# A scratch of rotated queries and keys laid out row by row, with six loads a half-head where there were ten

## The chip, the cores and the metric

The kernel runs on one core of a Trainium2 chip. The metric is device time in microseconds (us) from start to end of one execution, as a median of several. The core has five engines that run side by side, each through its own list of instructions in a fixed order: PE (TensorE, matrix products), DVE (VectorE), ACT (ScalarE), POOL (GpSimd) and SP (SyncE). In this kernel SP does no arithmetic: it issues every transfer between the chip's large memory (DRAM here) and the on-chip buffers, one after another. The transfers themselves run on 16 DMA engines. PE writes into eight accumulation banks that ACT and DVE read out.

## What is computed

One decoder layer over 1024 positions of width 2048, in float32. After a norm, one projection gives the columns of eight attention heads (queries, keys, values, gate) and of eight recurrent blocks. Each attention head has two score maps (m = 0, 1) of 64 dimensions, and the rotation acts on halves of 32 (t = 0, 1). Cut to what matters here:

```python
h = rms_norm(x, norm_gain[l]); proj = h @ w_in[l]
q, k, v, g_attn, xr, g_rec = jnp.split(proj, SPLITS, axis=-1)
q = rope(q.reshape(bsz, seq, 8, 2, 64), cos, sin)
k = rope(k.reshape(bsz, seq, 8, 2, 64), cos, sin)
s = einsum('bhmqd,bhmkd->bhmqk', q, k) * 64 ** -0.5      # causal
p = softmax(s); w = p[:, :, 0] - lam * p[:, :, 1]
o = w @ v; o = rms_norm(o, subln_gain) * 0.8 * silu(g_attn)
r = rg_lru(causal_conv(xr)) * silu(g_rec)
x = x + concat(o, r) @ w_out[l]
return rms_norm(x, final_gain)
```

To keep the precision of float32 in faster passes, the kernel splits each operand into a high and a low part (hi + lo) and adds up products of the parts.

## The kernel before

The class `Trunk` builds everything. It counts in slots: a slot (`tick`) is the work of one weight tile on PE, and generators that were spawned earlier (rope, scores, out_weights and so on) put their instructions into the slots as these go by. A scheduler then fixes the order on each engine, so neighbours can stand some places off from the order of the code; `order` fences below show the final one. Buffers are 89 tiles of 128 x 512 float32, handed out in turn.

There are three stages.

- **Projection** (`projection`, L659 on PE), to about 1100 us in the profile. In its last segment `rope(h, c4)` rotates queries and keys of head h. For each half l of the positions (512 columns) it ends with four tiles of 128 x 512: the high and low parts for t = 0 (`t2`, `t1`) and t = 1 (`pa`, `pb`). The 128 rows of each are four groups of 32: query m = 0, query m = 1, key m = 0, key m = 1. The four tiles are written whole to a scratch in DRAM, `fs[h, l]` of shape [4, 128, 512], in the order hi t0, hi t1, lo t0, lo t1 (L802).
- **Attention beside the recurrent half of the output projection** (`rec_half`), from about 1110 to 1745 us. The output projection runs 256 slots of three matmuls each (L1078, L1079, L1080: hi x hi, hi x lo, lo x hi), with weights that `out_weights` loads (L176, `b<-w_out`), copies on ACT (L189) and subtracts on POOL (L190). Between the slots, `scores` and `weighted` do the attention of 16 half-heads (8 heads, 2 halves of the positions). `head_load(h, l)` brings a half-head's operands in: keys k (2 tiles), queries q (4 tiles) and values (2 tiles). `score` multiplies them (L869, L870), DVE masks (L874), ACT takes the exponential (L881), PE turns the weights (L996), ACT and DVE split them (L1005, L1006), and PE applies them to the values (L1018, L1020, L1021). `head_out` norms the result (L967, L975, L978).
- **The attention half of the output projection** (`att_half`), to the end.

What each score tile holds matters for the change. The contraction of a score runs over 128 rows, which is four blocks of 32. The key tile of map m holds (hi t0, hi t1, lo t0, lo t1), block after block. The first query tile holds (hi t0, hi t1, hi t0, hi t1) and the second (lo t0, lo t1, lo t0, lo t1); L869 takes the first and L870 adds the second, so that all four products of parts are summed. A query tile is filled by two loads, each of 64 rows.

All transfers are issued by SP in its one order, by `self.load` (its line is L176) and `self.store` (L180); a load whose target tile is still being read waits there, and so does everything behind it. Besides, a transfer takes one of eight counters in turn and waits until the one eight places ahead of it on that counter has landed.

Of the kernel before, what the change touches and what calls it, by code (L numbers as in the profile page):

```python
# [13 lines left out]
F32 = mybir.dt.float32  # L14
# [7 lines left out]
P = 128  # L22
# [3 lines left out]
HALF = 512  # L26
# [95 lines left out]
class Trunk:  # L122
# [659 lines left out]
    def rope(self, h, c4):  # L782
        nc = self.nc
        for l in range(2):
            pa, pb = c4.pop(f"1{l + 1}"), c4.pop(f"2{l + 1}")
            t1, t2 = self.alloc(), self.alloc()
            sin, cos = self.sin[l], self.cos[l]
            self.tt(t1.f, pa.f, cos, ALU.mult)
            self.tt(t2.f, pb.f, sin, ALU.mult)
            yield 1  # L790
            self.tt(t1.f, t1.f, t2.f, ALU.subtract)
            self.split(t1.f, t2, t1)
            yield 2
            self.tt(pa.f, pa.f, sin, ALU.mult)
            self.tt(pb.f, pb.f, cos, ALU.mult)
            yield 2
            self.tt(pb.f, pb.f, pa.f, ALU.add)
            self.split(pb.f, pa, pb)
            yield 2
            fs = self.fs[h, l] = self.dram.tile([4, P, HALF], F32, name=self.nm("fs"))  # L800
            for i, b in enumerate((t2, pa, t1, pb)):
                nc.sync.dma_start(fs[i], b.f)  # L802
            self.rel(t1, t2, pa, pb)
            yield 2

# [30 lines left out]
    def head_load(self, h, l):  # L836
        k, q, v = [], [], []
        for m in range(2):
            kk = self.allocr()
            self.load(kk.f, self.fs[h, l][:, 64 + 32 * m:96 + 32 * m, :])  # L840
            k.append(kk)
        for i in (0, 2):
            for m in range(2):
                t = self.allocr()
                for j in range(2):
                    self.load(t.f[64 * j:64 * j + 64], self.fs[h, l][i:i + 2, 32 * m:32 * m + 32, :])
                q.append(t)
        for d in self.vsc[h, l]:
            t = self.allocr()
            self.load(t.f, d)  # L850
            v.append(t)
        self.hd[h, l] = (k, q, v)
# [382 lines left out]
```

## Time and profile before

| | us |
|---|---|
| median of 3 runs (1943.13 to 1944.86) | 1944.32 |
| profiled execution, its own time | 1941.15 |
| its span, first to last instruction | 1939.4 |
| PE busy / DVE busy / ACT busy / POOL busy | 1600.9 / 1273.9 / 815.3 / 632.7 |
| stretch 1110 to 1745 us (attention) | 635 |

Times in rows of the profile are microseconds of the profiled execution, from its first instruction. "Busy" is the time in which an engine has an instruction running; PE's matmuls are pipelined, so a busy PE is not one at its peak, and the clock column shows how much of TensorE's full clock was granted (1.00 is 2.4 GHz, 0.50 is 1.2 GHz). "DMA share" is the mean busy share of the 16 DMA engines. A wait is put down to the instruction whose completion ended it. "SPq" is the SP queue; its duration is how long SP was held by a transfer's issue, not how long the bytes took.

### The profile page before, as it was taken

The page shows a single profiled execution, that of the slowest core. Times are in us where ns is not written, and L with a number is a line of the kernel's source. Part 1 is how long each engine was busy: PE and PEld are TensorE (multiplying, and loading weights), DVE is VectorE, ACT ScalarE, POOL GpSimd, SP SyncE. Part 2 cuts the span into 40 slices and gives each one's busy share as a digit, 9 for nine tenths or more (in the row PEclk, how much of TensorE's full clock was granted, in tenths as well). Part 3 has the DMA queues.
Part 4 walks back from the last instruction along what each step waited for, and adds up shares of the span by engine and source line. Part 5 has one row for each costly group of instructions (what it writes and reads, how often), then busy time and mean ns, then how long its engine had stood idle before and what let it go on. Part 6 is the DMA issues. An engine that isn't in the chain of part 4 may idle for free. (4 is left out here: it accounts for less than half of the span.)

```text
span 1939.4 us, 22308 instructions
## 1 busy us (share of the span) xinstructions
PE 1600.9 (83%) x7140; PEld 1296.3 (67%) x7140; DVE 1273.9 (66%) x2120; ACT 815.3 (42%) x1462; POOL 632.7 (33%) x486
## 2 busy tenths in 40 slices
PE   7988988989889889999999945664857777599998
PEld 5767877767677667777777734553645556477876
DVE  9776798777887878989999823443634455373412
ACT  6444445453454455333333312333433343364442
POOL 3574323332333345232343310211211122147381
PEclk9999999999899899999999967787969788799999
DMA  6766423233232337455555724434444434455552
GB/s 240 250 209 217 160 81 123 90 125 112 85 122 90 111 104 268 166 188 177 197 204 190 253 87 149 137 134 144 148 160 141 136 103 141 130 178 169 184 197 87
DMA packets 164565, 299.98 MB, mean 155 GB/s; under 512 B 17376, under 2 KB 19552, under 8 KB 164448
## 3 DMA queue, kind: packets, MB, share of 16 engines
q1 hardware_dynamic: 164448, 298.56, 46.1%
q8 instruction: 56, 0.92, 0.2%
q14 instruction: 61, 0.50, 0.1%
HBM read 206.22 MB, written 92.27 MB: 154 GB/s over the span
## 5 line engine op out<-in xcount | busy, mean ns | idle before, releaser
L659 PE MATMUL pp<-b,b 128*128 128x512 f32 x3612 | 886.2, 403 | 104.8 <-DVE b L193 84.9
L659 PEld LDWEIGHTS pp<-b,b 128*128 128x128 f32 x3612 | 697.9, 195 | 275.2 <-DVE b L193 99.8
L190 POOL TENSOR_TENSOR b<-b,b 128x512 fp32r<-128x512 f32 x288 | 452.4, 1584 | 772.8 <-ACT b L189 437.4
L189 ACT CAST b<-b 128x512 fp32r<-128x512 f32 x592 | 355.1, 619 | 725.4 <-DVE b L193 277.9
L190 DVE TENSOR_TENSOR b<-b,b 128x512 fp32r<-128x512 f32 x304 | 243.3, 812 | 66.0 <-ACT b L189 56.8
L193 DVE TENSOR_TENSOR b<-b,b 128x512 f32<-128x512 f32 x340 | 256.3, 768 | 19.1 <-POOL b L190 12.4
L1078 PE MATMUL pq<-b,b 128*128 128x512 f32 x512 | 211.0, 412 | 19.1 <-ACT b L189 18.6
L1079 PE MATMUL pq<-b,b 128*128 128x512 f32 x512 | 209.7, 410 | 2.9 <-POOL b L190 2.8
L1080 PE MATMUL pq<-b,b 128*128 128x512 f32 x512 | 208.9, 408 | 3.0 <-DVE b L190 3.0
L193 DVE TENSOR_TENSOR b<-pp,b 128x512 f32<-128x512 f32 x215 | 146.9, 683 | 61.0 <-PE pp L659 48.2
L193 POOL TENSOR_TENSOR b<-b,b 128x512 f32<-128x512 f32 (+1 forms) x56 | 74.9, 1338 | 282.0 <-ACT b L733 89.8
L193 DVE TENSOR_TENSOR b<-pq,b 128x512 f32<-128x512 f32 x89 | 61.0, 686 | 150.6 <-PE pq L1080 125.1
L874 DVE CUSTOM_DVE_ANT_0 sw<-sw,mask 128x256 f32<-128x256 f32 (+7 forms) x128 | 97.0, 763 | 66.2 <-PE sw L870 64.8
L1006 DVE TENSOR_TENSOR b<-pq,b 128x512 fp32r<-128x512 f32 (+1 forms) x80 | 50.7, 634 | 118.4 <-ACT b L1005 117.3
L881 ACT ACTIVATE wide<-sw,mx 128x256 f32<-128x256 f32 (+7 forms) x128 | 93.8, 739 | 79.2 <-DVE mx L877 78.8
L1078 PEld LDWEIGHTS pq<-b,b 128*128 128x128 f32 x512 | 100.7, 197 | 36.5 <-ACT b L189 19.9
L1018 PE MATMUL pq<-b,b 128*128 128x256 f32 x160 | 51.5, 322 | 77.2 <-ACT b L1005 43.4
L1079 PEld LDWEIGHTS pq<-b,b 128*128 128x128 f32 x512 | 100.6, 196 | 21.4 <-POOL b L190 5.4
L1080 PEld LDWEIGHTS pq<-b,b 128*128 128x128 f32 x512 | 100.2, 196 | 21.1 <-DVE b L190 4.6
L193 DVE TENSOR_TENSOR b<-b,wide 128x512 f32<-128x512 f32 x120 | 99.0, 839 | 9.6 <-ACT wide L1148 9.0
L659 PE MATMUL pq<-b,b 128*128 128x512 f32 x420 | 103.8, 393 | 1.3 <-POOL b L190 1.0
L869 PE MATMUL sw<-b,b 128*128 128x512 f32 (+2 forms) x192 | 76.9, 402 | 28.4 <-ACT wide L881 21.9
(148 smaller groups left out, 1638.9 us busy)
## 6 DMA issues: line engine op xcount, KB each, us to landing
b<-w_in SPq DMA_DIRECT2D x192, 256.0 KB
b<-w_out SPq DMA_DIRECT2D x128, 256.0 KB
pt<-b SPq DMA_DIRECT2D x96, 256.0 KB
b<-pt SPq DMA_DIRECT2D x96, 256.0 KB
b<-xt SPq DMA_DIRECT2D x72, 256.0 KB
fs<-b SPq DMA_DIRECT2D x64, 256.0 KB
b<-fs SPq DMA_DIRECT2D x128, 128.0 KB
b<-yd SPq DMA_DIRECT2D x32, 256.0 KB
```

Source lines behind the costliest of these rows:

```text
L189: self.nc.scalar.copy(hi.r, x)
L190: (eng or self.nc.vector).tensor_tensor(out=lo.r, in0=x, in1=hi.f, op=ALU.subtract)
L193: (eng or self.nc.vector).tensor_tensor(out=out, in0=a, in1=b, op=op)
L659: nc.tensor.matmul(acc, lhsT=a.r[:, s], rhs=b.r, start=FIRST[pi] and qq == 0 and j == 0, stop=qq == 3 and j == 2, skip_group_check=True)
L869: nc.tensor.matmul(o, lhsT=q[m].r[:, qs], rhs=kk, start=True, stop=False)
L874: nc.vector.tensor_tensor_reduce(out=s, in0=s, in1=self.mask[:, 896 - off:896 - off + cols], scale=1.0, scalar=NEG, op0=ALU.add, op1=ALU.m ...
L881: nc.scalar.activation(p[:, :cols], self.swide[m][:, :cols], AF.Exp, scale=QK ** -0.5, bias=mx[:, m:m + 1], accum_out=sm[:, m:m + 1])
L1006: nc.vector.tensor_tensor(out=wl.r[:, first:], in0=self.tr[:, first:], in1=wh.f[:, first:], op=ALU.subtract)
L1018: nc.tensor.matmul(o, lhsT=vh.r[:, vs], rhs=wh.r[:, cs], start=(k2 == 0 and i == 0), stop=False)
L1078: nc.tensor.matmul(acc, lhsT=mh.r[:, s], rhs=wh.r, start=kt == 0, stop=False)
L1079: nc.tensor.matmul(acc, lhsT=mh.r[:, s], rhs=wl.r, start=False, stop=False)
L1080: nc.tensor.matmul(acc, lhsT=ml.r[:, s], rhs=wh.r, start=False, stop=kt == 7)
```

## The change

The scratch of a half-head gets the shape [4, 32, 6, 512]: first the group (query m = 0, query m = 1, key m = 0, key m = 1), then the row within the group, then a place for up to six blocks side by side. The four tiles go to places 0 to 3 of all four groups (four stores of 128 rows, each row of 2 KB now 12 KB from the next), and the two high tiles once more to places 4 and 5 of the query groups (two further stores of 64 rows). A half-head is then loaded by six transfers of 128 rows: each key tile reads places 0 to 3 of its group, the first query tile of a map places 0 to 3 and the second places 2 to 5, so that 4 x 512 numbers that lie in one run in DRAM become four neighbouring rows on the chip. The rows of a contraction are thus interleaved (row, block) where they were (block, row), in keys and queries alike. The first query tile now holds hi and lo beside the keys' hi and lo, the second lo and hi: the same four products are summed, in other pairs.

```diff
-            fs = self.fs[h, l] = self.dram.tile([4, P, HALF], F32, name=self.nm("fs"))
+            fs = self.fs[h, l] = self.dram.tile([4, 32, 6, HALF], F32, name=self.nm("fs"))
             for i, b in enumerate((t2, pa, t1, pb)):
-                nc.sync.dma_start(fs[i], b.f)
+                nc.sync.dma_start(fs[:, :, i].rearrange("g r c -> (g r) c"), b.f)
+            for i, b in enumerate((t2, pa)):
+                nc.sync.dma_start(fs[:2, :, 4 + i].rearrange("g r c -> (g r) c"), b.f[:64])
             self.rel(t1, t2, pa, pb)
...
         for m in range(2):
             kk = self.allocr()
-            self.load(kk.f, self.fs[h, l][:, 64 + 32 * m:96 + 32 * m, :])
+            self.load(kk.f, self.fs[h, l][2 + m, :, :4])
             k.append(kk)
         for i in (0, 2):
             for m in range(2):
                 t = self.allocr()
-                for j in range(2):
-                    self.load(t.f[64 * j:64 * j + 64], self.fs[h, l][i:i + 2, 32 * m:32 * m + 32, :])
+                self.load(t.f, self.fs[h, l][m, :, i:i + 4])
                 q.append(t)
```

On the DRAM side, the access pattern of a key load goes from 4 steps of 32 rows of 512 to 32 steps of 4 rows of 512; that of a query load from 2 steps of 32 rows (64 rows in all) to 32 steps of 4 (128 rows). The new stores have 128 or 64 steps of one row.

The instructions on PE, DVE, ACT and POOL are the same in number and kind; the scheduler shifts some of them by a few places in the attention stage. SP changes as follows. First the stores of head 0 in the projection, on SP, before (fs is the scratch, pt partial results, vs values):

```order
L802 DMA fs_6768<-b_6725 128x512
L802 DMA fs_6768<-b_6724 128x512
L176 DMA b_6819<-pt_2562 128x512
L176 DMA b_6815<-w_in 128x512
L176 DMA b_6817<-w_in 128x512
L176 DMA b_6851<-pt_2584 128x512
L802 DMA fs_6768<-b_6499 128x512
L802 DMA fs_6768<-b_6669 128x512
L180 DMA vs_6791<-b_6519 128x512
```

And now:

```order
L802 DMA fs_6768<-b_6725 128x512
L804 DMA fs_6768<-b_6725 64x512
L802 DMA fs_6768<-b_6724 128x512
L176 DMA b_6817<-w_in 128x512
L176 DMA b_6821<-pt_2562 128x512
L176 DMA b_6819<-w_in 128x512
L176 DMA b_6853<-pt_2584 128x512
L802 DMA fs_6768<-b_6499 128x512
L802 DMA fs_6768<-b_6669 128x512
L804 DMA fs_6768<-b_6499 64x512
L180 DMA vs_6793<-b_6519 128x512
```

The two stores of 64 rows (L804) stand between the others, each by the store of the same tile.

Second, the loads of one half-head in the attention stage, on SP, before; x is the residual input, ys a stored sum of the output projection, ms a stored head output, and "x2" marks two rows that follow each other (it is the head load that the trace has at 1248.83 us):

```order
L176 DMA b_10212<-x 128x512
L176 DMA b_10225<-fs_7380 128x1x512
L176 DMA b_10227<-fs_7380 128x1x512
L176 DMA b_10229<-fs_7380 64x1x512 x2
L176 DMA b_10232<-fs_7380 64x1x512 x2
L176 DMA b_10235<-fs_7380 64x1x512 x2
L176 DMA b_10238<-fs_7380 64x1x512 x2
L176 DMA b_10241<-vs_7552 128x512
L176 DMA b_10243<-vs_7553 128x512
L180 DMA ys_10211<-b_10093 128x512
L180 DMA ms_10209<-b_10155 128x512
L176 DMA b_10331<-w_out 128x512
```

And now:

```order
L176 DMA b_10228<-x 128x512
L176 DMA b_10241<-fs_7388 128x1x512
L176 DMA b_10243<-fs_7388 128x1x512
L176 DMA b_10245<-fs_7388 128x1x512
L176 DMA b_10247<-fs_7388 128x1x512
L176 DMA b_10249<-fs_7388 128x1x512
L176 DMA b_10251<-fs_7388 128x1x512
L176 DMA b_10253<-vs_7564 128x512
L176 DMA b_10255<-vs_7565 128x512
L176 DMA b_10343<-w_out 128x512
L176 DMA b_10357<-w_out 128x512
L176 DMA b_10370<-w_out 128x512
```

Eight loads of 64 rows have become four of 128, the weights stand behind the values as before, and the stores of ys and ms have moved behind the weights.

## Rows read from the trace of the kernel before

**Rows 1.** The page: its span, and in 40 equal slices of 48.5 us PE's busy share and the granted clock, in tenths.

```profile
span 1939.4 us, 22308 instructions
...
PE   7988988989889889999999945664857777599998
...
PEclk9999999999899899999999967787969788799999
```

**Rows 2.** Stretches of the span: bounds and length in us, then busy us and number of instructions of PE, PEld (weight loads), DVE, ACT and POOL, granted clock, DMA share, GB/s. First the last segment of the projection, then the attention stage, then four stretches of it in which PE is hardly ever idle, then one in which SP issues loads from fs and nothing else, last one in which the loads are the recurrent half's operands and weights.

```profile
806.00:1110.00 304.00, 289.21 (x1258) 232.90 (x1257) 281.56 (x426) 109.32 (x191) 96.87 (x47) 0.98 0.60 202
1110.00:1745.00 635.00, 419.96 (x2127) 342.86 (x2126) 288.58 (x751) 237.13 (x487) 123.48 (x148) 0.81 0.41 139
1360.00:1397.00 37.00, 36.72 (x212) 31.03 (x210) 27.22 (x73) 20.41 (x43) 8.47 (x12) 1.00 0.48 162
1570.00:1604.00 34.00, 32.30 (x187) 26.97 (x186) 25.49 (x60) 20.99 (x41) 11.10 (x12) 1.00 0.38 125
1616.00:1647.00 31.00, 29.81 (x166) 24.08 (x165) 22.11 (x64) 16.31 (x38) 8.94 (x11) 0.96 0.36 119
1690.00:1740.00 50.00, 49.16 (x270) 40.15 (x269) 36.36 (x97) 32.41 (x68) 14.90 (x14) 0.96 0.47 154
1255.20:1269.60 14.40, 14.40 (x77) 12.44 (x76) 10.19 (x23) 4.78 (x11) 1.48 (x2) 0.83 0.14 55
1090.00:1110.00 20.00, 19.14 (x87) 15.53 (x86) 17.47 (x25) 7.20 (x12) 7.95 (x7) 1.00 0.96 331
```

**Rows 3.** Whom PE waited for from 1110 to 1745 us, longest first: total us, times, longest us.

```profile
PE pq L1018 <- ACT b L1005: 43.4, 4, 18.7
PE pq L978 <- DVE hs L975: 38.0, 2, 27.6
PE pq L996 <- DVE b L1006: 24.3, 5, 12.0
PE sw L869 <- ACT wide L881: 21.9, 9, 9.3
PE pq L1018 <- issue: 21.3, 2, 10.9
PE pq L1078 <- ACT b L189: 18.2, 2, 18.0
PE sw L870 <- DMA b<-fs: 16.8, 3, 10.6
PE pq L1018 <- POOL b L1004: 12.3, 1, 12.3
PE sw L869 <- DMA b<-fs: 6.1, 2, 4.1
```

**Rows 4.** The timeline around 1191 to 1217 us, of SP (three rows), ACT and PE: start and duration in us, then the instruction, its count and in brackets the idle time before it and what ended it.

```profile
1191.95 9.50 SPq L176 DMA_DIRECT2D b<-fs  x3
1201.55 2.92 SPq L176 DMA_DIRECT2D b<-vs  x2
1204.52 1.74 SPq L176 DMA_DIRECT2D b<-w_out  x3
...
1215.70 1.87 ACT L189 CAST b<-b 128x512 fp32r<-128x512 f32 x3 [18.30 <-DMA b<-w_out]
...
1216.37 0.80 PE L1078 MATMUL pq<-b,b 128*128 128x512 f32 x1 [17.96 <-ACT b L189]
```

**Rows 5.** The chain of work that ended last, between 1190 and 1290 us: start, length in us, what. A DMA's piece runs from its issue to its landing.

```profile
1205.16 11.15 DMA b<-w_out
...
1241.53 10.81 DMA b<-vs
...
1262.15 2.44 SPq L176
1264.63 2.44 SPq L176
...
1274.58 9.70 DMA b<-w_out
```

**Rows 6.** The timeline of SP at the head load of the order fence above.

```profile
1248.83 20.74 SPq L176 DMA_DIRECT2D b<-fs  x10
1269.61 2.97 SPq L176 DMA_DIRECT2D b<-vs  x2
```

**Rows 7.** Issues on SP by the tensor they move: count, then the time that an issue held SP in ns (least, median, longest) and the us at which the first and the last started. Loads from fs, stores to fs, stores of the output and loads of x; the last two move 128 rows of 2 KB that lie 8 KB apart in DRAM.

```profile
L176 SPq DMA_DIRECT2D b<-fs x160: 484/993/4552, 1110.2 to 1669.4; - x160
L802 SPq DMA_DIRECT2D fs<-b x64: 319/320/1192, 806.8 to 1098.5; - x64
...
L1165 SPq DMA_DIRECT2D out<-b x32: 332/391/1256, 1828.6 to 1935.2; - x32
...
L176 SPq DMA_DIRECT2D b<-x x32: 327/382/1342, 1109.6 to 1691.3; - x32
```

**Rows 8.** The third matmul of a slot (L1080) alone, in the attention stage and in its four dense stretches: length, PE busy us and count, PEld, clock, DMA share, GB/s.

```profile
1110.00:1745.00 635.00, 108.12 (x257) 51.81 (x256) 0.81 0.41 139
1360.00:1397.00 37.00, 10.24 (x26) 4.89 (x26) 1.00 0.48 162
1616.00:1647.00 31.00, 7.96 (x19) 3.72 (x19) 0.96 0.36 119
1690.00:1740.00 50.00, 12.53 (x30) 6.02 (x31) 0.96 0.47 154
1570.00:1604.00 34.00, 7.97 (x20) 3.84 (x21) 1.00 0.38 125
```

## The prediction

> **What bounds the kernel now.** I read the slices of the page first [rows 1]. PE is busy nine tenths of nearly every slice of the projection and of the end, but only four to eight tenths of most slices between about 1110 and 1745 us, and there the granted clock falls with it. So one stage is ill, the attention stage, and it is the one that loads from fs. By stretches [rows 2] it lasts 635 us with PE busy 420 us, DVE 289, ACT 237, POOL 123, the DMA engines 0.41: on average nothing is full. The average hides two conditions. In four stretches of together 152 us PE is busy 148 us, at a clock of 0.96 to 1.00. Elsewhere it stands still: the nine longest kinds of wait [rows 3] add up to 202 us, with single waits of 10 to 28 us, under many names (ACT, DVE, POOL, "issue").
>
> One of them shows what is behind the names [rows 4, 5]. SP is held 9.5 us by three loads from fs, then 2.9 us by two of values, and only then, at 1204.5, issues weights. These land 11.15 us after their issue; ACT, which must copy them, has been idle 18.3 us, and PE 17.96 us behind ACT. The neighbouring pieces of the chain have the same form: values land after 10.8 us, weights after 9.7. Why loads from fs hold SP: each half query tile, 128 KB, takes 2.44 us [rows 5], and the ten loads of a half-head hold it for 20.7 us [rows 6], against 0.32 to 0.39 us for the median of other transfers [rows 7]. While only these run, the DMA share is 0.14 and 55 GB/s move [rows 2]: 0.14 x 16 = 2.2 engines. The other 14 are idle, though the engines can be had at a share of 0.96 and 331 GB/s (same rows). So a load of 64 rows whose DRAM side has 2 outer steps uses about two engines, and whatever is issued behind it waits for those two. Ten loads of 2.44 us are 24 us a half-head and 390 us in 16, in a stage of 635. That is what bounds it: two of 16 DMA engines, and SP held behind them.
>
> The Trainium skill, page "DMA: Bandwidth & Descriptors", has two statements on this that disagree here. Section "Rules for kernel authors" says two transfers to disjoint partition halves both spray over all 16 engines; that would make each half query load cheap, and the change nearly worthless. The trace speaks against it: 2.2 engines busy. Section "Why a DMA increments its semaphore by 16 and not by 1" says the number of engines is the largest up to 16 that divides the slowest dimension of both sides, which gives 2 for the half tiles, 4 for the key loads and 16 for the new ones (32 rows against 128). The trace agrees for the first; the last no run shows yet.
>
> **The change part by part.**
>
> *The loads.* 16 x 10 loads become 16 x 6, of the same bytes (1.5 MB a half-head). The new form, 32 outer steps on the DRAM side, stands nowhere in the trace. Its bounds: spread over all 16 as x and weights are, 256 KB at the 331 GB/s of [rows 2] take 0.8 us, six 4.8 us; confined to four engines, 256 KB take as long as 128 KB on two, 2.44 us, six 14.6 us. I take the first, because its outer step count of 32 is nearest to the 128 of the loads of x, which hold SP 0.38 us [rows 7], and far from the 2 of the slow ones. A half-head then asks for some 5 us of the engines instead of holding two for 24.
>
> *What the stage is without these holds.* I count progress in two ways, by PE's instructions and by slots, and apply the pace of the four dense stretches. PE instructions: 212 + 187 + 166 + 270 = 835 in 152 us, 5.49 a us; the stage has 2127, so 387 us [rows 2]. Slots: 26 + 20 + 19 + 30 = 95 in 152 us, 0.625 a us; 257 make 411 us [rows 8]. The two differ since the mix of attention and slots differs between stretches; I take the middle, 399. A check by subtraction: 635 less 202 of waits is 433; a mean clock of 0.81 means 241 us at the 1.2 GHz level, of which at most 202 were idle, so at least 39 us of work at half speed would take 20 less: 413 or below. The three agree within 26 us. PE is the bound there (148 of 152 us busy), DVE next with 111.
>
> *What comes back.* At the start of the stage PE waits directly for the first loads (6.1 us in the last row of [rows 3], and part of the 16.8 above it), and loads must still come in behind the 0.96 share of 1090 to 1110 us. I leave 15 us for that and for collisions, a choice; zero to 100 is possible. When a half-head's 2 MB come at once, a weight behind them waits some 6 us, less than a weight's lead of five slots (5 / 0.625 = 8 us), which hides it. Over the stage the engines go from a share of 0.41 to 0.41 x 635 / 414 = 0.63; the projection's last segment runs at 0.60 with PE busy 289 of 304 us [rows 2], so that much doesn't hold PE.
>
> *The stores.* 32 more issues at 0.32 us are 10 us of SP, and 4.2 MB more at 331 GB/s 13 us of the engines, spread over the 304 us of the projection's last segment, share 0.60 to 0.64. PE is hidden from it by loads of weights that are issued slots ahead; if that cover went, up to 13 us. The stores' rows now lie 12 KB apart. The nearest rows are stores of the output and loads of x, 8 KB apart: 0.39 and 0.38 us against 0.32 [rows 7], so 64 x 0.07 = 4 us of SP. I take zero for all of it, and 0 to 13 for the range. What stands behind the extra stores on SP is weights and partial results, each issued well before use.
>
> *Moved on SP.* Stores of ys and ms stand behind weights in places: they free buffers a few issues later, at 0.4 us each, against 89 buffers. Nothing.
>
> *Sum.* 399 + 15 = 414 for the stage, 221 less than 635. The profiled execution took 1941.15 us (span 1939.4), so 1720; the median of the runs is 3.2 us above the profiled execution, so 1723.
>
> **Rivals.**
>
> *Four engines.* The new loads are confined to four, at 14.6 us a half-head. The hold shrinks by 40%, and with it, in proportion, the loss of 236 us: 94 gained, 1850. For it: engines are plainly tied to the shape of the access. Against: the loads of x, whose outer steps are many, show nothing of it.
>
> *Another wait takes the place.* Loads that land together, or attention's own chain from PE over DVE and ACT and back, hold PE for half of what was lost: 118 gained, 1826. For it: most waits in [rows 3] name ACT or DVE. Against: in the dense stretches, some of which have loads from fs in flight, the same chain leaves PE busy 148 of 152 us.
>
> *It doesn't do what it says.* The 2.44 us are a price of the bytes between fs and the chip, whatever the shape: the same 1.5 MB take the same 24 us, and 1944 stays. Against: loads of other tensors, twice as large, hold SP a sixth as long. The rule on disjoint halves that the Trainium skill has (page "DMA: Bandwidth & Descriptors", section "Rules for kernel authors") leads to the same time.
>
> *Slower: rows far apart are the slow form.* The old loads took rows from blocks 256 KB apart, the old stores were one run. If distance and not the number of steps confines a transfer to two engines, the new loads of 256 KB take 4.9 us, six 29 us a half-head against 24, and the new stores of 256 KB 4.9 us each, 64 x 4.9 + 32 x 2.44 = 390 us of two engines inside 304 us of projection: some 90 us there and 50 in attention, about 2085. It decides from the point at which a store holds SP over 3 us. Against: output and x, 8 KB apart, hold it 0.4.
>
> **How the numbers follow.** The forecast has 0.80, four engines 0.06, another wait 0.07, no effect 0.04, slower 0.03. The forecast's own bounds: the densest stretch's pace, 212 instructions in 37 us, gives 371 us for the stage and, with no remainder, 1680; with 79 us more than the sum it is 1800, where the second rival begins. The range is 1685 to 1800. What a measurement of this kernel can tell from no change is about 0.2%, 4 us. Faster by more: 0.94 (forecast, four engines, another wait, and a little of no effect); within: 0.03; slower: 0.03.
>
> **What would show it.** Right: loads from fs hold SP under 1 us each; no stretch of SP's fs loads alone with a DMA share near 0.14; the waits of PE in the stage fall from 202 us to below 40; its mean clock rises from 0.81 to above 0.95; the stage lasts 390 to 440 us; the projection and the end (1745 to 1939) keep their length within 5 us. Wrong: issues at 2.4 us (four engines); PE waits over 100 us under ACT or DVE while loads land in 3 us (another wait); stores (L802, L804) holding SP over 1 us at the median, with a longer projection (the slower case).

## The result

The changed kernel takes 1712.76 us (median of 4 runs, 1709.47 to 1719.18) where the kernel before took 1943.72 in the same comparison: a ratio of 0.8818, with a 95% interval of 0.8788 to 0.8848. Forecast were 1723 us and a range of 1685 to 1800. The profiled execution after took 1714.92 us, its span is 1713.1.

The page of the changed kernel: span, PE's busy share and the granted clock in 40 slices, now of 42.8 us. They answer to [rows 1].

```profile
span 1713.1 us, 22261 instructions
...
PE   6888999898998988899899999989999999999997
...
PEclk9998999999999998999999999999999999999999
```

The hole in PE's row between the projection and the end is closed, and the clock no longer falls there. The stretches of the changed kernel, with columns as in [rows 2]: last segment of the projection, attention, end, and the four microseconds of one half-head's loads.

```profile
806.00:1110.00 304.00, 289.37 (x1270) 232.99 (x1269) 284.86 (x428) 109.33 (x191) 94.73 (x47) 0.99 0.66 216
1110.00:1520.00 410.00, 383.69 (x2121) 311.50 (x2120) 296.27 (x750) 236.93 (x486) 122.04 (x147) 0.99 0.64 214
1521.00:1713.00 192.00, 179.31 (x803) 147.28 (x803) 56.16 (x91) 74.50 (x157) 101.54 (x78) 0.97 0.48 163
1164.00:1168.00 4.00, 4.00 (x25) 3.49 (x24) 4.00 (x9) 1.52 (x3) 1.03 (x2) 1.00 0.86 280
```

In 410 us PE does 2121 of the 2127 instructions that took 635 us before. DVE and ACT do the same work as before in less time, the DMA engines work at 0.64 instead of 0.41. While a half-head's loads are issued, 0.86 of the engines are busy, where it was 0.14. The first segment has not become longer: the first load from fs is issued at 1110.5 us, before at 1110.2 [rows 7].

Whom PE waits for from 1110 to 1530 us; this answers to [rows 3].

```profile
PE pq L997 <- DVE wide L890: 14.3, 12, 2.8
PE sw L870 <- ACT wide L882: 7.0, 10, 2.2
PE pq L1081 <- DVE b L190: 2.8, 3, 1.2
PE pq L997 <- DVE b L1007: 1.7, 4, 0.6
```

The waits shown add up to 25.8 us, those of all rows to 28.0, none longer than 2.8. All but 3.4 us are on attention's own chain; the others are for a low part (L1081) and a load of x. (The line numbers are one higher than before.) SP at one half-head, which answers to [rows 6]:

```profile
1163.39 3.82 SPq L176 DMA_DIRECT2D b<-fs  x6
1167.31 1.02 SPq L176 DMA_DIRECT2D b<-vs  x2
1168.42 0.38 SPq L176 DMA_DIRECT2D b<-x  x1
```

Six loads hold SP 3.8 us where ten held it 20.7, and values and x follow at once. All issues that touch fs (which answer to [rows 7]), with the time from issue to landing of those from and to fs together:

```profile
L176 SPq DMA_DIRECT2D b<-fs x96: 512/547/867, 1110.5 to 1451.3; - x96
L802 SPq DMA_DIRECT2D fs<-b x64: 319/320/668, 808.3 to 1097.4; - x64
L804 SPq DMA_DIRECT2D fs<-b x32: 445/452/1634, 808.7 to 1099.7; - x32
...
DMA to landing us min/median/max: 2.0/3.9/6.9
```

And the weights of the output projection in the changed kernel: issue, who waited for them, time to landing.

```profile
L176 SPq DMA_DIRECT2D b<-w_out x128: 327/382/1212, 1091.7 to 1639.1; - x128
...
  ACT b L189: 18.5, 14
...
DMA to landing us min/median/max: 2.5/4.4/7.5
```

A weight lands 4.4 us after its issue at the median and 7.5 at most; before, the chain had pieces of 9.7 and 11.15 [rows 5].

### The profile page after: what moved, and what is told of

Its sections match the earlier page's. It is cut to its first block, busy times and chain, and to the rows that moved or that the text cites. A ratio compares the mean times of both kernels' runs of the same rounds, so it can differ in the third digit from the quotient of the medians.

```text
span 1713.1 us, 22261 instructions
## 1 busy us (share of the span) xinstructions
PE 1568.0 (92%) x7140; PEld 1268.1 (74%) x7140; DVE 1281.2 (75%) x2120; ACT 815.5 (48%) x1462; POOL 629.7 (37%) x486
## 5 line engine op out<-in xcount | busy, mean ns | idle before, releaser
L189 ACT CAST b<-b 128x512 fp32r<-128x512 f32 x592 | 355.0, 619 | 549.9 <-DVE b L193 275.4
L1080 PE MATMUL pq<-b,b 128*128 128x512 f32 x512 | 204.2, 399 | 2.3 <-POOL b L190 1.6
L1081 PE MATMUL pq<-b,b 128*128 128x512 f32 x512 | 203.6, 398 | 2.8 <-DVE b L190 2.8
L1079 PE MATMUL pq<-b,b 128*128 128x512 f32 x512 | 203.2, 398 | 0.1
L1081 PEld LDWEIGHTS pq<-b,b 128*128 128x128 f32 x512 | 96.9, 190 | 20.1 <-DVE b L190 4.2
L1080 PEld LDWEIGHTS pq<-b,b 128*128 128x128 f32 x512 | 96.7, 189 | 19.3 <-POOL b L190 4.3
L1079 PEld LDWEIGHTS pq<-b,b 128*128 128x128 f32 x512 | 96.8, 189 | 16.4 <-ACT b L189 0.5
L659 PE MATMUL pq<-b,b 128*128 128x512 f32 x420 | 103.5, 392 | 0.5 <-POOL b L190 0.5
L659 PEld LDWEIGHTS pq<-b,b 128*128 128x128 f32 x420 | 79.3, 189 | 17.5 <-POOL b L190 0.9
L1006 ACT CAST b<-pq 128x512 fp32r<-128x512 f32 (+1 forms) x80 | 43.5, 543 | 77.7 <-PE pq L997 74.7
L870 PE MATMUL sw<-b,b 128*128 128x512 f32 (+2 forms) x192 | 70.9, 372 | 7.4 <-ACT wide L882 7.0
```

Source lines behind the costliest of these rows:

```text
L189: self.nc.scalar.copy(hi.r, x)
L659: nc.tensor.matmul(acc, lhsT=a.r[:, s], rhs=b.r, start=FIRST[pi] and qq == 0 and j == 0, stop=qq == 3 and j == 2, skip_group_check=True)
L870: nc.tensor.matmul(o, lhsT=q[m].r[:, qs], rhs=kk, start=True, stop=False)
L1006: nc.scalar.copy(wh.r[:, first:], self.tr[:, first:])
L1079: nc.tensor.matmul(acc, lhsT=mh.r[:, s], rhs=wh.r, start=kt == 0, stop=False)
L1080: nc.tensor.matmul(acc, lhsT=mh.r[:, s], rhs=wl.r, start=False, stop=False)
```

## The experiments

The theory is that of the prediction: the number of outer steps on the DRAM side sets how many DMA engines a transfer gets, all such loads fall on the same few engines, and what stands behind them is late. Its rivals say that the number of loads, the distance of rows in DRAM or the bytes themselves cost the time.

**Old scratch, other order of steps.** The stores, the layout and all distances stay as before the change; only the order in which a load walks through blocks and rows is turned, in twelve loads of 64 rows.

```diff
-            self.load(kk.f, self.fs[h, l][:, 64 + 32 * m:96 + 32 * m, :])
+            for j in range(2):
+                s = self.fs[h, l][2 * j:2 * j + 2, 64 + 32 * m:96 + 32 * m, :]
+                self.load(kk.f[64 * j:64 * j + 64], s.rearrange("i r c -> r i c"))
...
-                    self.load(t.f[64 * j:64 * j + 64], self.fs[h, l][i:i + 2, 32 * m:32 * m + 32, :])
+                    s = self.fs[h, l][i:i + 2, 32 * m:32 * m + 32, :]
+                    self.load(t.f[64 * j:64 * j + 64], s.rearrange("i r c -> r i c"))
```

> Scratch and stores as before the change (blocks 256 KB apart, 64 stores), twelve loads of 64 rows a half-head, but the access pattern of each steps over the 32 rows first and the 2 blocks second. Theory (the number of outer steps on the DRAM side sets how many DMA engines a load uses): 32 steps use all 16, an issue holds SP about 0.5 us, twelve 6 us a half-head against 24; 1713 to 1730 us. Rival (rows far apart in DRAM are the slow form): 2.44 us a load as before, twelve 29 us; 1944 or slower. Rival (the number of loads is what costs): twelve instead of ten, 1944 or slower.

Measured: 1715.99 us, ratio to before 0.8835 (0.8812 to 0.8858). The whole gain is there without the new layout, with more loads than before, and with rows 256 KB apart. That leaves neither the number of loads nor the distance as the cause. The issues in this kernel:

```profile
L176 SPq DMA_DIRECT2D b<-fs x192: 507/596/1709, 1102.5 to 1448.1; - x192
```

**Six loads with four steps.** The other part of the change alone: six loads instead of ten and the high blocks stored twice, but whole blocks kept one behind the other.

```diff
-            fs = self.fs[h, l] = self.dram.tile([4, P, HALF], F32, name=self.nm("fs"))
+            fs = self.fs[h, l] = self.dram.tile([6, P, HALF], F32, name=self.nm("fs"))
             for i, b in enumerate((t2, pa, t1, pb)):
                 nc.sync.dma_start(fs[i], b.f)
+            for i, b in enumerate((t2, pa)):
+                nc.sync.dma_start(fs[4 + i, :64], b.f[:64])
...
+            self.load(kk.f, self.fs[h, l][:4, 64 + 32 * m:96 + 32 * m, :])
...
+                self.load(t.f, self.fs[h, l][i:i + 4, 32 * m:32 * m + 32, :])
```

> Six loads of 128 rows a half-head as after the change, with the high blocks stored twice, but the scratch keeps whole blocks of 128 rows (6 blocks, all stores in one run), so each load has 4 outer steps of 32 rows. Theory (outer steps set the engines): four engines, 2.44 us for 256 KB, six 14.6 us a half-head against 24.4; the loss of 230 us shrinks in proportion to 138: about 1850 us, DMA share near 0.27 while only these loads run. Rival (the number of loads costs): 1713 to 1720. Rival (price of the bytes): 1944.

Measured: 1816.36 us, ratio 0.9357 (0.9341 to 0.9374). Number and size of the loads are those of the changed kernel, 104 us are missing. A stretch of this kernel in which SP issues only such loads, columns as in [rows 2]:

```profile
1393.00:1398.00 5.00, 5.00 (x27) 4.13 (x26) 3.59 (x14) 1.80 (x6) 0.00 (x0) 0.89 0.26 102
```

0.26 x 16 is 4.2 engines and 102 GB/s, twice the 0.14 and 55 GB/s of two steps [rows 2]. The price in time was off, though: in proportion to 14.6 of 24.4 us I had 1850. (A variant below keeps this scratch and these loads and turns only the order of steps.)

**Queries alone, keys alone.** Each half of the loads of the kernel before is turned to rows first, the other left (here the queries; the key loads of the second run in the same way):

```diff
-                    self.load(t.f[64 * j:64 * j + 64], self.fs[h, l][i:i + 2, 32 * m:32 * m + 32, :])
+                    s = self.fs[h, l][i:i + 2, 32 * m:32 * m + 32, :]
+                    self.load(t.f[64 * j:64 * j + 64], s.rearrange("i r c -> r i c"))
```

> Before the change, with the query loads alone (eight of 64 rows) stepping over 32 rows first; key loads keep 4 outer steps. Query and key rows no longer pair, so the scores are other numbers; the work is the same. Theory: the queries' 19.5 us on two engines go, the two key loads stay on four engines at 2.44 us each, 4.9 us a half-head; in proportion a loss of 46 us stays: about 1760, between 1715 and 1765 as a hold this short may be hidden. Rival (rows far apart): 1944.

> Before the change, with the key loads alone (two of 128 rows) stepping over 32 rows first; the eight query loads keep 2 outer steps. Query and key rows no longer pair, so the scores are other numbers; the work is the same. Theory: eight loads on two engines stay, 19.5 us a half-head; in proportion a loss of 184 us stays: about 1897, 1870 to 1930. Rival (number of loads): 1944, no change.

Measured: 1723.85 us (ratio 0.8889, 0.8875 to 0.8902) with the queries turned, 1882.5 us (0.9703, 0.9672 to 0.9734) with the keys. Turning the queries gains 216 of the 224 us that turning both gained on the same chip, turning the keys 57. The two add up to more than the whole: the two key loads cost little by themselves, more where eight slow loads follow them. With the keys turned, a stretch of fs loads shows the two engines as before:

```profile
1241.60:1249.00 7.40, 7.40 (x44) 6.38 (x42) 5.38 (x16) 2.52 (x6) 0.20 (x1) 0.91 0.13 51
```

**Blocks apart, eight steps, and a first head earlier.** Three variants beside the changed kernel on the same chip. The first has six loads of 32 row steps from the scratch of whole blocks (`rearrange("i r c -> r i c")` on the loads of the four-step kernel). The second lays the changed scratch out in groups of four rows, so that a load has 8 outer steps (the stores follow the new shape):

```diff
-            fs = self.fs[h, l] = self.dram.tile([4, 32, 6, HALF], F32, name=self.nm("fs"))
+            fs = self.fs[h, l] = self.dram.tile([4, 8, 6, 4, HALF], F32, name=self.nm("fs"))
```

The third issues the first half-head's loads in `out_prefetch`, in the last unit of the projection:

```diff
+        elif i == 1:
+            self.head_load(0, 0)
...
     def scores(self):
-        self.head_load(0, 0)
```

> The changed kernel itself, to be compared on the same chip with the next three: 1708 to 1720 us.

> The changed kernel's number and size of loads and stores and its order of steps (32 rows first, then 4 blocks), but the four blocks of a row lie 256 KB apart in DRAM instead of side by side. Theory (the order of steps is what matters, neighbourhood isn't): within 0.3% of the changed kernel. Rival (side by side in DRAM brings part of the gain): slower than it by 5 us or more.

> The changed kernel with its scratch laid out in groups of 4 rows, so that a load has 8 outer steps (8 x 16 x 512) and a store 32 or 16. Theory (outer steps set the engines): eight engines, 256 KB in about 1.2 us, six 7.3 us a half-head. Between the 4.9 us of the queries-only kernel, which cost 11 us of time, and the 14.6 us of four steps, which cost 103: in line between them 34 us over the changed kernel, 1730 to 1755. Rival (anything above a few engines is as good): same as the changed kernel.

> The changed kernel with the first half-head's eight loads issued some six slots earlier, in the last unit of the projection, ahead of the loads of the recurrent operands. In the changed kernel PE idles or runs alone on attention's chain from about 1124 to 1140 us. If the late first loads cause this, 5 to 12 us less than the changed kernel; if it is the attention chain of DVE and ACT itself, no change.

Measured: the changed kernel 1711.19 us (ratio 0.8814, 0.8802 to 0.8826). Blocks 256 KB apart: 1713.24 (0.8826, 0.8814 to 0.8838), no difference that this shows; blocks side by side bring nothing of their own. This kernel differs from the one with four steps in the order of steps alone, 1713 us against 1816: the cleanest pair of all. Eight steps: 1729.1 (0.89, 0.8883 to 0.8917), 18 us more, half of the 34 expected and just under the range. No issue holds SP there:

```profile
L176 SPq DMA_DIRECT2D b<-fs x96: 577/582/788, 1109.9 to 1464.7; - x96
```

While only fs loads move, from 1151 to 1153 us, 0.53 x 16 = 8.5 engines are busy:

```profile
1151.00:1153.00 2.00, 2.00 (x14) 1.79 (x13) 1.68 (x3) 0.00 (x0) 0.00 (x0) 1.00 0.53 204
```

How the 18 us come about is not taken apart; the stores of this kernel hold SP longer as well, 0.52 us at the median. The first head early: 1706.81 (0.8792, 0.878 to 0.8804), the fastest of all kernels here, 4.4 us under the changed one and a little under the 5 to 12 expected; the two intervals just touch. From 1100 to 1145 us this kernel does 179 PE instructions,

```profile
1100.00:1145.00 45.00, 39.14 (x179) 30.65 (x179) 29.36 (x73) 16.77 (x41) 17.00 (x18) 0.96 0.80 290
```

and the changed one 151:

```profile
1100.00:1145.00 45.00, 36.16 (x151) 26.84 (x150) 27.04 (x65) 15.69 (x37) 16.85 (x18) 0.92 0.82 303
```

So part of the slow start seems to come from the late first loads, a gain at the edge of the noise.

**Stores with few steps.** The prediction's slower case put the stores on two engines, by their distance, at 4.9 us each. Here the number of steps puts them on few, at 2.44 us each by the theory. With 33 rows instead of 32 to a group, the groups are no longer evenly spaced, and the pattern of a store keeps 4 outer steps (2 for the stores of 64 rows); the loads are those of the changed kernel.

```diff
-            fs = self.fs[h, l] = self.dram.tile([4, 32, 6, HALF], F32, name=self.nm("fs"))
+            fs = self.fs[h, l] = self.dram.tile([4, 33, 6, HALF], F32, name=self.nm("fs"))
             for i, b in enumerate((t2, pa, t1, pb)):
-                nc.sync.dma_start(fs[:, :, i].rearrange("g r c -> (g r) c"), b.f)
+                nc.sync.dma_start(fs[:, :32, i], b.f)
```

> The changed kernel with its groups padded from 32 to 33 rows in the scratch, so that a store can no longer be read as one run of evenly spaced rows: the stores of 128 rows have 4 outer steps, those of 64 rows 2; the loads keep 32. This is the price that the prediction's slower case gave to the stores. Theory (outer steps set the engines for writes as well): 2.44 us each, 96 make 234 us of hold in the 304 us of the projection's last segment, where weights and partial results are issued some slots ahead; at a share of hold of 0.77 against attention's 0.61, the segment grows by 30 to 150 us, the attention stage not at all: 1740 to 1860. Rival (the rule holds for reads from DRAM alone): 1713.

Measured: 1871.15 us (0.9654, 0.9619 to 0.9689), some 160 us over the changed kernel, just above what I expected. It is writes as well as reads: from 851.5 to 855.5 us, behind the stores of a head, 0.13 x 16 = 2.1 engines are at work.

```profile
851.50:855.50 4.00, 1.59 (x8) 0.97 (x6) 1.91 (x4) 0.62 (x1) 0.00 (x0) 1.00 0.13 51
```

The issues of the stores, and from 806 to 1280 us the longest wait of SP's loads and of ACT:

```profile
L802 SPq DMA_DIRECT2D fs<-b x64: 509/539/4385, 807.3 to 1245.0; - x64
L804 SPq DMA_DIRECT2D fs<-b x32: 501/1960/4373, 808.1 to 1249.3; - x32
```

```profile
SPq L176 <- DMA fs<-b: 64.0, 19, 10.1
ACT b L189 <- DMA fs<-b: 153.9, 13, 17.1
```

The last store is issued at 1249 us instead of 1100: nearly all of the loss is in the projection. None of PE's waits there names fs (the largest in total, 70.9 us, is for DVE), but ACT's do: its copies wait 153.9 us for stores to fs, in the changed kernel 16.5 us from 806 to 1110 us, and DVE waits 137.1 us for these copies, there 1.4. So much of the loss reaches PE over ACT and DVE. That ACT waits for tiles which the stores still read is likely, but not shown.

**Who is late: weights on ACT's queue.** In the kernel before, the 128 loads of output weights are issued by ACT, so that they no longer stand behind fs loads on SP.

```diff
-                    self.load(raw.f, self.io["w_out"][cg, 8 * (1 - half) + kt])
+                    self.nc.scalar.dma_start(raw.f, self.io["w_out"][cg, 8 * (1 - half) + kt])
```

> Before the change, with the loads of the output weights (128) issued from ACT's queue instead of SP's: fs loads still hold SP and two engines, but weights no longer stand behind them on SP. Theory as read at 1192 to 1217 us (most of PE's waits come through late weights): the waits behind ACT's copies of weights go, those for x, fs and ys stay; 1780 to 1880. Rival (weights are late because the two engines are full, whichever queue asks): 1920 or more.

Measured: 1953.59 us, 0.8% slower than before (ratio 1.0081, 1.0052 to 1.011). My time was wrong, and the rival's reason was wrong as well. In the kernel before, waits for weights from 1110 to 1745 us were

```profile
  ACT b L189: 108.9, 13
```

and in this one, over the whole span,

```profile
  ACT b L1005: 16.0, 2
  ACT b L189: 10.0, 14
  ACT wide L1148: 2.0, 1
```

So weights do come in time from the other queue, though the two engines are as full as ever. One of them shows it: ACT issues a weight at 1224.68 us, while two fs loads hold SP for 5.6 us. From 1224.6 to 1229.6 us ACT's queue (q10) and SP's (q1) moved, in packets, MB and share of the 16 engines:

```profile
q10 hardware_dynamic: 144, 0.26, 17.3%
q1 hardware_dynamic: 113, 0.23, 11.6%
```

The whole weight went within 5 us, beside fs loads on 1.9 engines. On SP, a weight issued after the fs loads took 11.15 us [rows 5]. But the chain now runs through everything else that SP issues behind the fs loads:

```profile
1201.41 10.92 DMA b<-x
...
1229.64 13.66 DMA b<-fs
...
1263.96 11.46 DMA b<-vs
```

Values and fs loads had been late before as well [rows 3, 5]. And the run has a cost of its own. ACT now stands before its issues, and these rows are waits of ACT from 1110 to 1760 us, ended by transfers of which the copies named (L963 and L1005, which read PE's banks) read nothing:

```profile
ACT b L1005 <- DMA b<-w_out: 16.0, 2, 11.7
ACT b L963 <- DMA b<-fs: 15.9, 2, 12.6
ACT b L1005 <- DMA b<-vs: 13.8, 1, 13.8
ACT b L1005 <- DMA b<-fs: 11.9, 1, 11.9
```

In the kernel before, from 1110 to 1745 us, only the copies of L189 waited for a transfer. So how much of the loss the late weights made by themselves, this run doesn't show.

**Old loads on POOL's queue.** The counterpart: in the kernel before, the ten fs loads are issued by POOL in their old form, and SP keeps the rest.

```diff
-            self.load(kk.f, self.fs[h, l][:, 64 + 32 * m:96 + 32 * m, :])
+            self.nc.gpsimd.dma_start(kk.f, self.fs[h, l][:, 64 + 32 * m:96 + 32 * m, :])
```

(and the query loads in the same way)

> Before the change, with the ten fs loads of a half-head in their old form (4 and 2 outer steps) issued from POOL's queue instead of SP's. Nothing then stands behind them on SP; weights, values, x and stores share the DMA engines with them only by turns. If the hold of SP (and of whatever is queued behind it) is what costs: 1713 to 1780, with weights landing in 3 to 5 us though an fs load still takes its 2.4 us or longer. Rival (the engines that these loads fill make every other transfer late, whoever issues them): 1880 or more, weights still landing in 8 to 11 us.

Measured: 1775.87 us (0.9153, 0.9113 to 0.9193), 166 of the 230 us that the change gains. The loads from fs, their time to landing (with the stores), then the weights:

```profile
L846 POOL DMA_DIRECT2D b<-fs x128: 651/672/732, 1103.0 to 1514.2; - x128
...
L840 POOL DMA_DIRECT2D b<-fs x32: 683/698/827, 1099.0 to 1505.2; - x32
...
DMA to landing us min/median/max: 2.0/8.6/21.4
```

```profile
DMA to landing us min/median/max: 2.5/5.1/12.2
```

The fs loads still land late, up to 21 us, but weights on SP land after 5.1 us at the median. So fs loads that are late cost, by themselves, at most the other 64 us. But the edit changed more than the queue. From 1244 to 1248 us POOL's queue (q0), which moves these loads, had (packets, MB, share of the 16 engines)

```profile
q0 software_dynamic: 434, 0.46, 59.8%
```

0.46 MB in 4 us are 115 GB/s. From SP the same loads moved at 55 GB/s on two engines [rows 2], and loads with four steps at 102 GB/s on four. So the loads issued by POOL, taken together, ran on more than two engines. That most of the loss was what stood in SP's queue is borne out by this run and by the weight on ACT's queue above, but this run doesn't separate it from the two full engines. What makes the other 64 us (POOL's 0.67 us an issue, 160 times, beside its splits; late fs loads; engines shared) is not taken apart.

## Why the prediction was right

*What bounds the kernel.* That the number of outer steps sets the engines held in every run of SP's loads in which it was read. Engines in use were 2.2, 4.2, 8.5 and, in the changed kernel and beside other transfers, 13.8 (0.86) for 2, 4, 8 and 32 outer steps, with bytes and number of loads equal in the last three. That SP's queue behind them is the way to the loss is the best reading of the two runs with other queues, but neither separates it wholly from the full engines. That it was always the same two engines follows from [rows 2]: ten loads stood in line and still only 2.2 were busy. The Trainium skill, page "DMA: Bandwidth & Descriptors", section "Why a DMA increments its semaphore by 16 and not by 1", gives the largest number up to 16 that divides the slowest dimension on both sides; the traces agree, with 2.2, 4.2, 8.5 and, beside other transfers, 13.8 engines where that gives 2, 4, 8 and 16. Its section "Rules for kernel authors" (two transfers to disjoint halves use all 16) doesn't hold for these loads: 2.44 us and a share of 0.14.

*The loads.* I took 16 engines for the new form; the alternative of four was run and is 104 us slower.

*The stage.* Forecast 399 us by the pace of the dense stretches and 15 for what comes back, 414 together; the profiled execution needs about 411. Taking the pace from stretches of the same stage in which the fault was absent was what made the size come out: PE's mix, the clock and the chain of DVE and ACT are all in it. That it came within 3 us is partly luck: the 399 is the middle of two counts 24 us apart, and the 15 us was a choice. The waits that remain are 28 us, most of them of the kinds that the dense stretches had too, and of the late first loads 4 us could be had.

*The stores.* Nothing, as forecast: PE is busy 289.4 us from 806 to 1110 us, before 289.2. A store of 64 rows holds SP 0.45 us, not 0.32, and the strided ones of 128 rows 0.32, not 0.39: 14 us of SP in sum where I had 10 + 4, hidden all the same.

*The total.* The profiled execution came out at 1714.9 where the sum had 1720; 3 us of the difference are the stage, 2 the end (192 us, not 194). The other 5 us between 1723 and 1712.8 lie between profiled execution and median, which I had carried over from before as +3.2 and which is -2.2 now.

*The rivals.* Four engines: run and not what the change does; its price was 34 us too high. Another wait: 28 us of waits in the trace, not 100. No effect of the shape: refuted by four steps against 32. Distance: refuted by the old scratch with turned steps and by the blocks apart. Stores at few steps do cost, 160 us, so the slower case had a real price, though not by the distance it named; the point from which it decides was right in kind (issues of up to 4.4 us there, in the changed kernel 0.32 and 0.45 us at the median and 1.6 at most), and the change doesn't reach it because its stores are read as one run of 128 or 64 steps.

*What was wrong.* The loss is not proportional to the hold, as I had used for the rivals. In us of engine time a half-head against us over the changed kernel: 4.9 gave 12 (keys on four engines), 7.3 gave 18 (eight steps), 14.6 gave 104, 19.5 gave 170 and 24.4 gave 230 (the engine times are worked out from 2.44 us a load at two or four engines, half of that at eight). The first 7 us are nearly hidden, by loads issued slots ahead and by SP not being held at all (longest issue 0.86 us and 0.79 us in the first two); beyond that each us a half-head costs about 12, nearly the 16 of 16 half-heads in a row. These points come from different kernels on several chips, so they are a trend and no law. And the reading that PE's waits come through late weights was right for the wait I showed, but taking it out of SP's queue gained nothing: other loads stayed late there, and ACT stood before its own issues; how the two share is open. Two numbers of the range don't fit either: 79 us above 1723 are 1802, not 1800, and the forecast's own lower bound of 1680 lies below the range's 1685.

## What to carry to other kernels

When a transfer holds its queue far longer than others of its size, look at the DMA share while it runs alone: 0.14 or 0.26 of 16 engines is a shape, not a bandwidth. Write the access pattern with the many short rows as the outer steps on the DRAM side; here a turned order of steps alone, with the old layout, gave the whole gain. And price the cure by the pace of the same stage where the fault is absent, and a part cure not in proportion: here a short hold was nearly hidden, and of a long one three quarters were paid.

## What the runs showed of the hardware that was not expected

SP is not held from the first slow load on. In the kernel before, the ten loads of a half-head begin with issues of about 0.5 us, and only after the first few do most take 2.44 us; in the kernel with four steps, at least three issues pass at about 0.5 before it. In the kernel with two slow key loads a half-head, no issue is longer than 0.86 us, and it lost only 12 us. Loads issued by POOL were moved in other pieces: this kernel's page counts 195414 packets, 54368 of them under 512 bytes, where that of the kernel before, with the same loads on SP, has 164565 and 17376 for the same bytes.
